# First operands made in halves on two engines, and a scaling of the third tile behind the last tile's first y addition: a two-layer hybrid decoder on one NeuronCore

## The chip, the cores and the metric

The kernel runs on one core of one Trainium2 chip. The metric is the device time of one execution in microseconds (us); lower is better.

## What is computed

Two layers work on x, 512 tokens of 1024 features in float32. Each layer normalises x, projects it with one wide matrix into eight groups of columns, runs a gated linear recurrence (HGRN2, 8 heads of 128) on some groups and a causal sliding-window attention (16 query heads of 64, 2 key/value heads, window 128, a learned sink per head) on others, gates both with SiLU, projects the joined heads back, and adds the normalised result to x:

```python
h = rms_norm(x, g_pre)
proj = jnp.einsum('bsd,de->bse', h, w_in)
q_h, f_h, i_h, z_h, q_a, k_a, v_a, z_a = jnp.split(proj, SPLIT_POINTS, axis=-1)
o_h = hgrn2(q_h, f_h, i_h, lb)
o_h = rms_norm(o_h, g_head).reshape(B, S, HG_WIDTH) * jax.nn.silu(z_h)
...
o_a = sliding_window_attention(q_a, k_a, v_a, sinks) * jax.nn.silu(z_a)
y = jnp.einsum('bse,ed->bsd', jnp.concatenate([o_h, o_a], axis=-1), w_out)
return x + rms_norm(y, g_post)
```

## The kernel before

Tokens lie in four tiles of 128 (NT), features in eight pieces of 128 (KT). A float32 operand of a matmul is written as a high part, rounded to the fp32r type, and a low part, the rest; each product is made of three matmuls, high x high, low x high and high x low. For weights, ACT casts the piece to the high part (line 183) and DVE subtracts it to get the low part (line 184).

The program is written with a scheduler. It estimates when each instruction could start and orders each engine's instructions by it, except those wrapped in `pin`, which keep the order in which the code gives them. So an edit in one place can change the order in another. Beside it, `later(n, ...)` puts a piece of code behind n steps of the projections (a step is three matmuls, line 295), and `merge` mixes attention or the recurrence with the projections' steps.

**The start.** The first work is the key/value projection of layer 0, in `first_kv` (line 1040). SP loads in turn the transposed x (tile xs, eight pieces of 128 features, called xk(k)) and its weights (tile raw, four pieces, each for two k). For each pair of k, `high` (ACT) scales xs by the gain gcol into hhi, `whigh` (ACT) casts the weights, `low` and `wlow` (DVE) make the low parts, and `kv(k)` issues twelve matmuls of 256 columns (line 1067): four token tiles for each of the three products. Ahead of them three warm-up matmuls run on a tile of ones (line 1044; the tile u in the profile). Later the rotated keys, tile b, are copied on ACT (line 476) and transposed on PE (line 492).

**Attention** (lines 548 to 635) makes, for sixteen steps, scores on PE (559, 572), masks them and takes the maximum on DVE (577, 579), then the negated maximum negm (583), exponentials on ACT (590), sums and their reciprocal on DVE (594, 595), the scaling of the probabilities s on POOL (597), transposes on PE (603), masks on POOL (615), values on PE (629), and an addition into oa on DVE (635).

**The end.** The last projection of the last layer makes y for each token tile in two halves of 512 columns; in the last tile the second half is cut in two pieces of 256. For each piece DVE adds the matmuls' result to y (line 912), ACT squares it and sums the squares (954), and, for the first half, POOL multiplies y by the gain (956); for the second half DVE makes that product, yg, which is the tile s in the profile (961). When a tile's pieces are done, DVE adds up the sums (951, 354), POOL takes the reciprocal root r (356), and DVE scales and adds both halves to x (973, tile a), each followed by its store to the output (974, on SP, for one piece of the last tile on ACT). The function is `final` (line 932). The additions of line 912 carry a high priority for the scheduler.

## Time and profile before

| | |
|---|---|
| time, median of 3 runs | 908.9 us (907.81 to 909.1) |
| the profiled execution's own time | 907.05 us |
| its span | 905.3 us |
| granted TensorE clock, mean | 0.999 |
| PE busy | 893.1 us, 99% of the span |
| DVE, ACT, POOL busy | 652.1, 471.7, 255.4 us |
| moved by DMA | 102.82 MB, mean 114 GB/s |

The span is the time between the first and the last event of the profiled execution. PE is the matmul engine, PEld its weight loads, DVE, ACT and POOL the vector, scalar and GpSimd engines, SP the engine that issues most transfers. A row of the timeline gives the start and the duration in us, the engine, the line of the kernel, the operation, the tile written and those read, and, in brackets, how long the engine was idle just before and what released it. An operation named x2 or x8 stands for that many in one row. The durations of PE's rows are modelled and overlap; the spacing of their starts is what a matmul takes.

### The profile page before, as it was taken

The page shows a single profiled execution, that of the slowest core. Times are in us where ns is not written, and L with a number is a line of the kernel's source. Part 1 is how long each engine was busy: PE and PEld are TensorE (multiplying, and loading weights), DVE is VectorE, ACT ScalarE, POOL GpSimd, SP SyncE. Part 2 cuts the span into 40 slices and gives each one's busy share as a digit, 9 for nine tenths or more (in the row PEclk, how much of TensorE's full clock was granted, in tenths as well). Part 3 has the DMA queues.
Part 4 walks back from the last instruction along what each step waited for, and adds up shares of the span by engine and source line. Part 5 has one row for each costly group of instructions (what it writes and reads, how often), then busy time and mean ns, then how long its engine had stood idle before and what let it go on. Part 6 is the DMA issues. An engine that isn't in the chain of part 4 may idle for free.

```text
span 905.3 us, 18588 instructions
## 1 busy us (share of the span) xinstructions
PE 893.1 (99%) x7206; PEld 746.8 (83%) x7206; DVE 652.1 (72%) x1179; ACT 471.7 (52%) x1067; POOL 255.4 (28%) x233
## 2 busy tenths in 40 slices
PE   9999999999999999999999999999999999999997
PEld 7788888888888878888888888888888888888885
DVE  5878987989666885555787787877767557666556
ACT  6636767654656323534453376686346463145242
POOL 0135544204313123020332344550134121230102
PEclk9999999999999999999999999999999999999999
DMA  8783712332222222434356556222422322223413
GB/s 307 225 219 123 204 48 70 105 94 84 72 82 74 91 82 60 129 122 128 99 176 187 150 154 173 65 73 86 116 73 60 105 69 84 72 71 99 135 35 140
DMA packets 57145, 102.82 MB, mean 114 GB/s; under 512 B 6625, under 2 KB 9185, under 8 KB 57057
## 3 DMA queue, kind: packets, MB, share of 16 engines
q1 hardware_dynamic: 56768, 101.50, 37.0%
q8 instruction: 57, 0.93, 0.4%
q14 instruction: 32, 0.25, 0.1%
q10 hardware_dynamic: 288, 0.14, 0.1%
HBM read 89.03 MB, written 12.58 MB: 112 GB/s over the span
## 4 chain that ended last, share of the span: by engine, by line
PE 87%; DVE 6%; issue 3%; ACT 2%; POOL 1%; DMA 0%; POOLq 0%; DVEq 0%; ACTq 0%
PE pj L295 71%; PE ac L629 3%; PE sc L572 2%; PE sc L770 2%; PE ac L839 2%; PE sc L603 1%; PE ac L842 1%; PE ac L826 1%; DVE wlo L184 1%; PE sc L892 1%; PE sc L559 1%; PE sc L814 1%; PE ac L711 1%; DVE a L973 1%; DVE y L912 0%
## 5 line engine op out<-in xcount | busy, mean ns | idle before, releaser
L183 ACT CAST whi<-raw 128x512 fp32r<-128x512 f32 x256 | 155.5, 620 | 123.1 <-PE pj L295 112.4
L184 DVE TENSOR_TENSOR wlo<-raw,whi 128x512 fp32r<-128x512 f32 x253 | 182.0, 737 | 41.7 <-ACT whi L183 40.3
L295 PE MATMUL pj<-hhi,wlo 128*128 128x512 f32 x512 | 202.3, 396 | 0.0
L295 PE MATMUL pj<-hhi,whi 128*128 128x512 f32 x512 | 199.9, 390 | 0.0
L295 PE MATMUL pj<-hlo,whi 128*128 128x512 f32 x512 | 199.5, 390 | 0.0
L295 PE MATMUL pj<-whi,ops 128*128 128x512 f32 (+1 forms) x520 | 172.8, 395 | 0.2 <-DVE ops L872 0.2
L295 PEld LDWEIGHTS pj<-whi,ops 128*128 128x128 f32 x520 | 97.2, 188 | 19.8 <-DVE ops L872 0.6
L295 PEld LDWEIGHTS pj<-hhi,whi 128*128 128x128 f32 x512 | 96.1, 188 | 20.6
L295 PEld LDWEIGHTS pj<-hhi,wlo 128*128 128x128 f32 x512 | 96.2, 188 | 19.4
L295 PEld LDWEIGHTS pj<-hlo,whi 128*128 128x128 f32 x512 | 96.2, 188 | 19.0
L295 PE MATMUL pj<-whi,hlo 128*128 128x512 f32 x256 | 102.9, 404 | 0.0
L295 PE MATMUL pj<-wlo,ops 128*128 128x512 f32 (+1 forms) x260 | 100.8, 388 | 0.5 <-ACT ops L871 0.5
L295 PE MATMUL pj<-wlo,hhi 128*128 128x512 f32 x256 | 100.3, 392 | 0.3 <-DVE wlo L184 0.3
L295 PE MATMUL pj<-whi,hhi 128*128 128x512 f32 x256 | 100.2, 391 | 0.0
L789 POOL TENSOR_TENSOR k<-k,tot 128x512 f32<-128x512 f32 x40 | 58.3, 1480 | 108.3 <-PE sc L770 51.9
L590 ACT ACTIVATE s<-sc,negm 128x128 f32<-128x128 f32 x128 | 45.5, 368 | 36.9 <-DVE negm L583 34.7
L295 PEld LDWEIGHTS pj<-wlo,ops 128*128 128x128 f32 x260 | 49.0, 188 | 9.6 <-ACT ops L871 0.9
L295 PEld LDWEIGHTS pj<-whi,hhi 128*128 128x128 f32 x256 | 48.0, 188 | 10.3
L295 PEld LDWEIGHTS pj<-wlo,hhi 128*128 128x128 f32 x256 | 48.3, 189 | 8.6 <-DVE wlo L184 0.8
L295 PEld LDWEIGHTS pj<-whi,hlo 128*128 128x128 f32 x256 | 48.2, 188 | 8.0
L788 DVE TENSOR_TENSOR q<-q,tot 128x512 f32<-128x512 f32 x40 | 37.4, 946 | 20.3 <-PE sc L774 10.9
L597 POOL TENSOR_TENSOR s<-s,sums 128x512 f32<-128x512 f32 x32 | 35.2, 1100 | 51.6 <-DVE sums L595 27.7
(211 smaller groups left out, 1392.0 us busy)
## 6 DMA issues: line engine op xcount, KB each, us to landing
raw<-in_win_dram SPq DMA_DIRECT2D x192, 256.0 KB, 2.7
raw<-in_wout_dram SPq DMA_DIRECT2D x64, 256.0 KB, 2.7
stack<-rot SPq DMA_DIRECT2D x16, 512.0 KB, 3.4
qs<-stack SPq DMA_DIRECT2D x32, 256.0 KB, 4.6
xs<-in_xt_dram SPq DMA_DIRECT2D x8, 256.0 KB, 5.3
raw<-in_wkv_dram SPq DMA_DIRECT2D x8, 256.0 KB, 3.6
a<-in_x_dram SPq DMA_DIRECT2D x8, 256.0 KB, 3.7
x_mid<-a SPq DMA_DIRECT2D x8, 256.0 KB, 3.3
```

The source lines that it names most:

```text
L183: keep(nc.scalar.copy(hi, v))
L184: keep((nc.gpsimd if i in on_pool and i % 2 else nc.vector).tensor_tensor(lo, v, hi.bitcast(F32), op=ALU.subtract))
L295: nc.tensor.matmul(u.o, lhsT=u.sta(k, u.w)[i], rhs=u.mov(k, u.w)[j], start=(n == 0), stop=(n == len(u.list) - 1))
L559: pin(nc.tensor.matmul(S[:, h * P:(h + 1) * P], lhsT=q[:, h, t_], rhs=kst[v][p][:, 0:P], start=(h == 0 and p == 0), stop=(h == 3 and p == 1)))
L572: pin(nc.tensor.matmul(S[:, h * 256:(h + 1) * 256], lhsT=q[:, 2 * hp_ + h, t_], rhs=kst[v][p][:, (n - 1) * P:(n + 1) * P], start=(h == 0 a ...
L590: nc.scalar.activation(pt[:, h * P:(h + 1) * P], cur[h], AF.Exp, bias=negm[:, h:h + 1], scale=SCALE, accum_out=sums[:, h:h + 1])
L597: nc.gpsimd.tensor_tensor(pv, pv, sums.unsqueeze(2).broadcast_to([P, 4, P]), op=ALU.mult)
L629: pin(nc.tensor.matmul(U, lhsT=vst[v][:, blk, :], rhs=d, start=(i == 0), stop=(i == len(terms) - 1)))
L770: pin(nc.tensor.matmul(L[32 * b:32 * b + 32, c:c + 16], lhsT=k[:, o_ + 32 * b:o_ + 32 * b + 32], rhs=qv[:, blk:blk + qu, 1, :], start=True ...
L788: nc.vector.tensor_tensor(qv[:, :, 1, :], qv[:, :, 1, :], tv[:, :, 0].unsqueeze(2).broadcast_to([P, 2 * nb, hh]), op=ALU.mult)
L789: nc.gpsimd.tensor_tensor(kv_[:, :, 0, :], kv_[:, :, 0, :], tv[:, :, 1].unsqueeze(2).broadcast_to([P, 2 * nb, hh]), op=ALU.mult)
L839: pin(nc.tensor.matmul(O[:, c], lhsT=A[:, c], rhs=vs(j, n), start=(n == 0), stop=False))
```

## The change

At the start, for k = 0 alone: hhi is made in two halves of 256 tokens by DVE (`tensor_scalar`), the weights' high part in two halves of 256 columns by ACT. For the first pair of k, the order of the matmuls is high x high of both k, and then the other two products of each. The warm-up is two matmuls of 512 columns, not two and a half, and reads a tile of ones of 128 columns repeated four times; that tile is filled first on DVE, ahead of mhalf. At the end, for the third tile (tt == NT - 2) of the last layer, the second scaling and its store are put behind five further steps with `later`, and pinned.

```diff
-            for i, (c, v, e, w) in enumerate(parts):
+            def put(i, c, v, e, w):
                 xs = xt[c][:, e:e + w]
-                (pin if not last else lambda ins: ins)(nc.vector.scalar_tensor_tensor(xs, v[:, e:e + w], r, xs, op0=ALU.mult, op1=ALU.add))
+                (pin if not last or (tt == NT - 2 and i) else lambda ins: ins)(nc.vector.scalar_tensor_tensor(xs, v[:, e:e + w], r, xs, op0=ALU.mult, op1=ALU.add))
...
+            for i, part in enumerate(parts):
+                if last and tt == NT - 2 and i:
+                    later(5, None, lambda e=(i, *part): put(*e))
+                else:
+                    put(i, *part)
...
+    ones = tmp("u")
+    nc.vector.memset(ones[:, 0:P], 1.0)
     mhalf = const.tile([P, 4], F32, name="mhalf")
...
-    ones = tmp("u")
-    nc.vector.memset(ones, 1.0)
...
-        for n in (512, 512, 256):
-            pin(nc.tensor.matmul(warm[:, 0:n], lhsT=ones[:, 0:P], rhs=ones[:, 0:n], start=True, stop=True))
+        for _ in range(2):
+            pin(nc.tensor.matmul(warm, lhsT=ones[:, 0:P], rhs=ones[:, 0:P].unsqueeze(1).broadcast_to([P, 4, P]), start=True, stop=True))
...
-        def kv(k):
-            for i, j in ((0, 0), (1, 0), (0, 1)):
+        def kv(k, pairs=((0, 0), (1, 0), (0, 1))):
+            for i, j in pairs:
...
+        conv[0] = tuple(big.tile([P, 512], F32R, tag="v", name="wkv", bufs=8) for _ in range(2))
+        for c in (slice(0, 256), slice(256, 512)):
+            pin(nc.vector.tensor_scalar(hhi[:, 0, c], xk(0)[:, c], gcol[:, 0:1], None, op0=ALU.mult))
+            pin(nc.scalar.copy(conv[0][0][:, c], raws[0][:, c]))
         for j in range(KT // 2):
-            high(2 * j)
-            whigh(j)
+            if j:
+                high(2 * j)
+                whigh(j)
             low(2 * j)
             high(2 * j + 1)
             wlow(j)
             low(2 * j + 1)
-            kv(2 * j)
-            kv(2 * j + 1)
+            if j:
+                kv(2 * j)
+                kv(2 * j + 1)
+            else:
+                for k in range(2):
+                    kv(k, [(0, 0)])
+                for k in range(2):
+                    kv(k, [(1, 0), (0, 1)])
```

The scheduler's order changes in three stretches: at the start, between the first projections and the middle of layer 0's attention, and at the end. Elsewhere, and on SP throughout, it is the same.

PE, where the rotated keys are transposed (line 492; pj is the PSUM tile of a projection, the numbers name single tiles). Before:

```order
L295 MATMUL pj_481<-hhi_121,whi_398 128x512
L295 MATMUL pj_543<-hhi_121,wlo_405 128x512
L295 MATMUL pj_543<-hlo_122,whi_404 128x512
L492 MATMUL sc2_80<-ident_110,b_498 128x128 x4
L492 MATMUL sc0_78<-ident_110,b_498 128x128 x4
L295 MATMUL pj_543<-hhi_121,whi_404 128x512
L295 MATMUL pj_543<-hhi_121,wlo_411 128x512
```

The same place of the changed kernel, in which all tile numbers from here on are one higher:

```order
L295 MATMUL pj_482<-hhi_121,whi_399 128x512
L295 MATMUL pj_544<-hhi_121,wlo_406 128x512
L295 MATMUL pj_544<-hlo_122,whi_405 128x512
L295 MATMUL pj_544<-hhi_121,whi_405 128x512
L492 MATMUL sc2_80<-ident_110,b_499 128x128 x4
L492 MATMUL sc0_78<-ident_110,b_499 128x128 x4
L295 MATMUL pj_544<-hhi_121,wlo_412 128x512
```

The projection's high x high matmul has moved ahead of the transposes; its weights are those of the matmul before it.

DVE, in the attention stage of layer 0, near 88 to 93 us of the profile (sc are score tiles, mx, negm, ds and sums the small values of a step, wlo a low weight part). Before:

```order
L583 SCALAR_TENSOR_TENSOR negm<-mx,nsnk 128x4
L184 TENSOR_TENSOR wlo<-raw,whi 128x512
L586 TENSOR_TENSOR ds<-snk,negm 128x4
L342 TENSOR_TENSOR a<-sc_80,a 128x512
L577 COPY_PREDICATED sc_78<-masks,sc_78 128x2x128
L184 TENSOR_TENSOR wlo<-raw,whi 128x512
L579 TENSOR_REDUCE mx<-sc_78 128x2
L577 COPY_PREDICATED sc_79<-masks,sc_79 128x2x128
L594 TENSOR_TENSOR sums<-sums,es 128x4
L635 TENSOR_TENSOR oa<-ac_82,u 64x2x128
L579 TENSOR_REDUCE mx<-sc_79 128x2
L595 RECIPROCAL sums<-sums 128x4
```

And in the changed kernel:

```order
L184 TENSOR_TENSOR wlo<-raw,whi 128x512
L583 SCALAR_TENSOR_TENSOR negm<-mx,nsnk 128x4
L635 TENSOR_TENSOR oa<-ac_81,u 64x2x128
L586 TENSOR_TENSOR ds<-snk,negm 128x4
L342 TENSOR_TENSOR a<-sc_80,a 128x512
L184 TENSOR_TENSOR wlo<-raw,whi 128x512
L577 COPY_PREDICATED sc_78<-masks,sc_78 128x2x128
L594 TENSOR_TENSOR sums<-sums,es 128x4
L579 TENSOR_REDUCE mx<-sc_78 128x2
L577 COPY_PREDICATED sc_79<-masks,sc_79 128x2x128
L595 RECIPROCAL sums<-sums 128x4
L635 TENSOR_TENSOR oa<-ac_82,u 64x2x128
```

A wlo has moved ahead of negm, and the reciprocal ahead of the addition into oa and of the second maximum.

DVE at the end of the program (y the result, s the product yg, ss the sums of squares, r the root of the third tile). Before:

```order
L973 SCALAR_TENSOR_TENSOR a<-y,r_9996,a 128x512
L973 SCALAR_TENSOR_TENSOR a<-s,r_9996,a 128x512
L912 TENSOR_TENSOR y<-pj,y 128x512
L912 TENSOR_TENSOR y<-pj,y 128x256
L961 TENSOR_TENSOR s<-y,b 128x256
L912 TENSOR_TENSOR y<-pj,y 128x256
L951 TENSOR_TENSOR ss<-ss 128x1
```

In the changed kernel:

```order
L973 SCALAR_TENSOR_TENSOR a<-y,r_9997,a 128x512
L912 TENSOR_TENSOR y<-pj,y 128x512
L973 SCALAR_TENSOR_TENSOR a<-s,r_9997,a 128x512
L912 TENSOR_TENSOR y<-pj,y 128x256
L961 TENSOR_TENSOR s<-y,b 128x256
L912 TENSOR_TENSOR y<-pj,y 128x256
L951 TENSOR_TENSOR ss<-ss 128x1
```

The third tile's second scaling has changed places with the last tile's first y addition; nothing else has moved here.

## The prediction

> **What bounds the kernel now.** The page first: its span and its first part.
>
> ```profile
> span 905.3 us, 18588 instructions
> PE 893.1 (99%) x7206; PEld 746.8 (83%) x7206; DVE 652.1 (72%) x1179; ACT 471.7 (52%) x1067; POOL 255.4 (28%) x233
> ```
>
> PE is busy in 893.1 of 905.3 us. A change that removes no large matmul can only move the 12 us in which PE isn't busy, and waits that the pipelined records hide. So I read the chain that ended last, in order of time, and then who PE waits for.
>
> ```profile
> 26.83 3.64 DMA raw<-in_win_dram
> ...
> 42.87 1.09 PE sc L492 x8
> 43.96 14.12 PE pj L295 x62
> ```
>
> ```profile
> PE sc L492 <- ACT b L476: 0.8, 1, 0.8
> ...
> PE sc L572 <- ACT s L590: 0.5, 2, 0.3
> ```
>
> Up to 42.87 the chain runs through transfers and the small engines; from there it is PE's stream nearly without a break (62 matmuls in 14.12, 0.23 each), and at the very end, shown further down, it leaves PE for DVE, ACT and POOL. In the waits each row gives total, times and longest: before the L492 transposes PE waits 0.8 us once, behind attention's exponentials 0.5 in two waits. These are the places to watch. The timeline shows the first.
>
> ```profile
> 41.70 0.39 PE L295 MATMUL pj<-hlo,whi 128*128 128x512 f32 x1
> ...
> 42.19 0.62 ACT L476 COPY b<-b 128x512 f32<-128x512 f32 x1 [2.02 <-DVE b L475]
> ...
> 42.87 1.09 PE L492 MATMUL sc<-ident,b 128*128 128x128 f32 x8 [0.78 <-ACT b L476]
> ```
>
> PE stands still for 0.78 us until ACT's copy of b is done. Whatever PE gains before 41.70 lengthens this wait, and up to 0.78 us of PE's lateness shortens it, as long as b's own chain stays where it is.
>
> **The first operands.** PE weight loads and ACT in the first 10 us.
>
> ```profile
> 1.53 0.50 PEld L1044 LDWEIGHTS sc<-u 128*128 128x128 f32 x2 [1.53 <-DVE u L1035]
> ...
> 3.40 0.34 PEld L1044 LDWEIGHTS sc<-u 128*128 128x128 f32 x1 [0.52 <-issue]
> ...
> 4.26 0.34 PEld L1044 LDWEIGHTS sc<-u 128*128 128x128 f32 x1 [0.52 <-issue]
> ...
> 4.59 0.62 ACT L1058 CAST wkv<-raw 128x512 fp32r<-128x512 f32 x1
> ...
> 5.03 0.19 PEld L1044 LDWEIGHTS sc<-u 128*128 128x128 f32 x1 [0.43 <-issue]
> ...
> 5.26 0.62 PEld L1067 LDWEIGHTS ac<-wkv,hhi 128*128 128x128 f32 x4
> ...
> 7.04 0.72 ACT L1050 ACTIVATE hhi<-xs,gcol 128x512 fp32r<-128x512 f32 x1 [1.03 <-DMA xs<-in_xt_dram]
> ...
> 7.73 1.23 PEld L1067 LDWEIGHTS ac<-wkv,hhi 128*128 128x128 f32 x8
> 7.75 0.62 ACT L1058 CAST wkv<-raw 128x512 fp32r<-128x512 f32 x1
> ...
> 9.37 1.03 PEld L1067 LDWEIGHTS ac<-wkv,hhi 128*128 128x128 f32 x8
> ```
>
> Today the first kv matmul waits for the whole cast of wkv, 4.59 to 5.21. In halves, beside hhi on DVE, the first half is there after some 0.42 us (the 128x256 square on ACT, in the last block of rows below), so PE starts near 5.0, a quarter of a microsecond sooner. That doesn't last. ACT makes hhi of k=1 after both casts, 4.6 + 2 x 0.42 + 0.72 = 6.2; then 20 of the first 24 matmuls remain, at 0.12 each (eight loads in 1.03, so (1.03 - 0.19) / 7). They end at 8.6. The next four need hhi of k=2, which waits for its transfer until 7.04, and wkv's second piece, cast right behind it by 8.37; the eight loads from 7.73 take 1.23 and not 1.03 because they meet that. So PE goes on at 8.4 to 8.6 either way: between nothing and 0.2 us later. The DVE halves of hhi cost 0.43 each at most (the 128x256 product on DVE, 897.78 below) and run while wkv's piece is still under way; what follows them on DVE is due only behind the first eight matmuls. The shorter warm-up, two instructions for two and a half, frees about 0.9 us that PE then spends waiting. All of it lies ahead of 41.70, with 0.78 us of wait as cover: I take 0, bounds 0 and, should b's chain be disturbed too, +0.2 and -0.2.
>
> **The order that moves with it.** One 512-column matmul that stood behind the L492 transposes now stands before them, its operands already used by the matmul before it. It fills 0.23 us of the 0.78 (the spacing above): -0.23. The bounds are -0.23 and 0, the latter if b comes later by as much. In the attention stage DVE's order changes in a few places. This is the one where PE waits.
>
> ```profile
> 88.02 0.68 DVE L184 TENSOR_TENSOR wlo<-raw,whi 128x512 fp32r<-128x512 f32 x1
> ...
> 91.86 0.41 DVE L635 TENSOR_TENSOR oa<-ac,u 64x256 f32<-64x256 f32 x1
> ...
> 92.52 0.16 DVE L595 RECIPROCAL sums<-sums 128x4 f32<-128x4 f32 x1
> ```
>
> ```profile
> 92.85 1.04 POOL L597 TENSOR_TENSOR s<-s,sums 128x512 f32<-128x512 f32 x1 [3.20 <-DVE sums L595]
> ```
>
> ```profile
> 93.48 0.39 PE L295 MATMUL pj<-whi,hhi 128*128 128x512 f32 x1
> 93.95 0.66 PE L603 MATMUL sc<-ident,s 128*128 128x128 f32 x4
> ```
>
> The matmul at 93.48 leaves the array after 0.23, at 93.71; the transposes start at 93.95, when POOL's s is done (92.85 + 1.04 = 93.89): a hidden wait of 0.24. In the new order the reciprocal stands ahead of the oa addition and the reduction, worth 0.66 (91.86 to 92.52), more than the wait: -0.24. Against it, the 0.68 us wlo is now ahead of negm, so the exponentials start later; bound +0.45 (0.68 less the 0.24). I take -0.24, since the reciprocal in the row waits for DVE's own queue and not for ACT.
>
> **The end.** DVE, ACT and POOL over the last two tiles.
>
> ```profile
> 882.79 0.69 DVE L961 TENSOR_TENSOR s<-y,b 128x512 f32<-128x512 f32 x1
> ...
> 892.83 1.29 POOL L956 TENSOR_TENSOR y<-y,b 128x512 f32<-128x512 f32 x1 [2.95 <-ACT u L954]
> ...
> 893.68 1.00 DVE L961 TENSOR_TENSOR s<-y,b 128x512 f32<-128x512 f32 x1
> ...
> 896.06 0.75 DVE L973 SCALAR_TENSOR_TENSOR a<-s,r,a 128x512 f32<-128x512 f32 x1
> ...
> 896.73 1.02 DVE L912 TENSOR_TENSOR y<-pj,y 128x512 f32<-128x512 f32 x2
> ...
> 897.50 0.63 ACT L954 ACTIVATE u<-y 128x512 f32<-128x512 f32 x1 [3.05 <-DVE y L912]
> ...
> 897.78 0.43 DVE L961 TENSOR_TENSOR s<-y,b 128x256 f32<-128x256 f32 x1
> ...
> 898.31 1.27 POOL L956 TENSOR_TENSOR y<-y,b 128x512 f32<-128x512 f32 x1 [2.95 <-ACT u L954]
> 898.54 0.42 DVE L912 TENSOR_TENSOR y<-pj,y 128x256 f32<-128x256 f32 x1 [0.34 <-PE pj L295]
> 898.88 0.71 DVE L951 TENSOR_TENSOR ss<-ss 128x1 f32<-128x1 f32 x1
> 899.06 0.42 ACT L954 ACTIVATE u<-y 128x256 f32<-128x256 f32 x1 [0.29 <-DVE y L912]
> 899.38 0.19 ACT L954 ACTIVATION_READ_ACCUMULATOR u<-y 128x1 f32 x1
> ...
> 899.85 0.15 DVE L354 SCALAR_TENSOR_TENSOR s<-ss 128x1 f32<-128x1 f32 x1
> ```
>
> The third tile's scaling a<-s (896.06) now follows the y addition (896.73). The products it adds are ready: only 24 matmuls of 256 columns, 24 x 0.12, lie between them and PE's end near 898.5, so they were done by 895.7. The addition starts at 896.06 and everything it releases 0.67 sooner: the square at 896.83, POOL's y at 897.64 to 898.91. DVE's total is the same, so L961 of 256 columns is still due at 897.78. Here the rows warn. Where POOL multiplies y, DVE's L961 takes 1.00 and not 0.69: it ends at 894.68, 0.56 after POOL's end at 894.12, as if its 512 columns had only then begun; and L951, one column, lasts 0.71, until POOL's end at 899.58. The addition L912, with one operand in PSUM, takes its plain 0.42 amid POOL's y (898.54). So in these rows a DVE operation with both operands in SBUF stands still while POOL works. The SBUF page of the Trainium skill (section "SBUF: two separate sides") says it as a lock: of such a DVE operation and a POOL one, the first to start has the port pair and the other fully blocks. The trace agrees, with 0.71 us for one column; by that rule the side that starts second pays, and the sum below is what it comes to.
>
> Before, POOL's y met L951, and L354 began at 899.85. After, it meets L961, due 0.14 us after POOL starts: L961 ends at 898.91 + 0.28 = 899.2, and the last y addition, which came at 898.54 when PE was done, comes near 899.1. From its start to the end of the square's readout took 1.03 (898.54 to 899.57), so L354 begins at about 900.15: +0.30. What follows (root on POOL, three scalings, the last store) is as before. Nothing waits behind the moved scaling but these DVE steps; its store moves 0.67 later on SP, well ahead of the last tile's. Bounds: -0.25 if POOL and DVE didn't meet (L354 right behind the readout at 899.57), +0.6 if all of the 0.58 us by which the addition comes later stayed.
>
> **Sum:** 0 - 0.23 - 0.24 + 0.30 = -0.17. The profiled execution took 907.05 us, its span and 1.75 around it, so it would take 906.9. It lies 1.85 under the median of the three runs, 908.9; on that scale 908.7. The parts' bounds added, -0.92 and +1.25, make 908.0 to 910.2 on it. About 0.2%, or 1.8 us, is what a measurement of this kernel can tell from no change.
>
> **The rivals.**
>
> *A, faster by the whole cover:* the end meets no POOL operation (-0.25), the L492 wait goes whole because b comes sooner (-0.78), and the waits behind the exponentials go (-0.5): -1.5, or 907.4. For it: the order moves at all these places. Against: b's chain is untouched, and DVE and POOL overlap unless POOL slips by 0.14 us. 0.13.
>
> *B, slower through attention:* the wlo of 0.68 us that DVE now does ahead of negm at several steps delays exponentials, sums, POOL's s and the transposes. Where a step has no slack PE pays up to 0.68. It decides from the third such step on: 3 x 0.68 + 0.30 - 0.23 = +2.1, or 911.0. For it: at 93.71 PE already waits. Against: that wait is one of few, and the same order brings the reciprocal forward. 0.08.
>
> *C, the clock:* the loads show PE slow at first, 0.34 up to 4.26, then 0.19 at 5.03, 3.5 us after its first matmul. While slow, a 512-column pass takes 0.43 (two in 3.40 to 4.26), so 0.21 for 256 columns and not 0.12. Warm-up ends sooner now, and PE pauses between 4.5 and 6.2. If the clock stayed low for all 24 first matmuls they'd cost 24 x 0.09 = 2.2 us more, of which the wait at 41.70 absorbs 0.55: +1.6 or, with the sum, 910.3; above 0.2% from about five matmuls more. Against: PE's pause of 0.78 before 42.87 slows nothing after it, the 62 matmuls from 43.96 keep 0.23. The Trainium skill's page "TensorE: Matmul & The Clock Gate" (section "What's actually happening") has the clock open after one busy window of about 3.4 us whose phase is free. By that rule a warm-up of two instructions may miss a full window, which is this rival; the trace agrees with the 3.5 us, and no run here shows the phase. 0.05.
>
> *D, no effect:* the end is as before and the waits merely shift: 908.9. For it: most edits lie under cover. 0.14. That the scaling is not moved is excluded by the order.
>
> **How the numbers follow.** The forecast has 0.60, A 0.13, B 0.08, C 0.05, D 0.14. The likeliest is the forecast's 908.7. The three runs of before spread over 1.3 us, so the range is the forecast's 908.0 to 910.2 taken down to A's 907.4: 907.4 to 910.2, with B, half of C and a few mishaps outside. Faster by over 0.2% needs A and more, such as waits that the records hide: 0.06. Slower: B and half of C, 0.10. Within: 0.84.
>
> **What would show it.** Right: PE's first kv load near 5.0, but PE at k=2 still at 8.4 to 8.6; the wait before L492 near 0.55 or less; transposes near 94 without a gap; L961 of 256 columns lasting over 1 us beside POOL's y, and the last y addition waiting for DVE, some 0.5 us, and no longer for PE. Wrong: a slow weight load after 5.5, more PE waits behind exponentials between 60 and 110, or a last L354 that starts less than 1.31 us after PE's last release (898.54 to 899.85 now).

## The result, and where the time went

| | before | after |
|---|---|---|
| median, same chip, 12 runs each | 907.9 us (906.95 to 909.1) | 909.52 us (908.57 to 911.18) |
| ratio after to before | | 1.0021, 95% interval 1.0014 to 1.0028 |
| the profiled execution's own time | 907.05 us | 908.58 us |
| its span | 905.3 us | 906.9 us |

The change makes the kernel slower by 1.6 us in the median, 1.3 to 2.5 us by the interval; the two profiled executions differ by 1.53. The forecast of 908.7 us came from a loss at the end and two gains ahead of it. The loss at the end came within 0.04 us of the forecast; of the two gains the one in attention was outweighed several times over by a loss in the same place. (In the experiment called e3 below, two of the twelve executions took 2303 and 4339 us; its ratio leaves them out.) First the first part of the changed kernel's profile page, against the first fence of the prediction.

```profile
PE 894.4 (99%) x7204; PEld 746.4 (82%) x7204; DVE 653.1 (72%) x1181; ACT 471.9 (52%) x1067; POOL 255.1 (28%) x233
```

PE has two rows fewer (one warm-up matmul, which is listed as two) and is listed as busy for 1.3 us more; its rows can run on through short waits, as one further down does. So the sums don't show the loss. The waits of PE in the changed kernel (total, times, longest) do:

```profile
PE sc L572 <- ACT s L590: 1.2, 3, 0.7
...
PE sc L492 <- ACT b L476: 0.5, 1, 0.5
```

The wait before the L492 transposes fell from 0.8 to 0.5, as forecast. The waits behind attention's exponentials grew from 0.5 in two to 1.2 in three. To place the loss, take the same work of PE in both kernels and read when it starts. PE in the changed kernel:

```profile
4.94 1.83 PE L1073 MATMUL ac<-wkv,hhi 128*128 128x256 f32 x8
...
17.16 0.40 PE L295 MATMUL pj<-hhi,wlo 128*128 128x512 f32 x1
...
42.84 1.09 PE L492 MATMUL sc<-ident,b 128*128 128x128 f32 x8 [0.53 <-ACT b L476]
...
66.40 0.60 PE L603 MATMUL sc<-ident,s 128*128 128x128 f32 x4
...
94.54 0.39 PE L295 MATMUL pj<-whi,hhi 128*128 128x512 f32 x1
94.77 0.60 PE L603 MATMUL sc<-ident,s 128*128 128x128 f32 x4
...
899.47 0.28 PE L295 MATMUL pj<-whi,ops 128*128 128x256 f32 x1
```

The same landmarks in the kernel before, as far as the prediction doesn't show them:

```profile
17.16 0.40 PE L295 MATMUL pj<-hhi,wlo 128*128 128x512 f32 x1
...
66.67 0.60 PE L603 MATMUL sc<-ident,s 128*128 128x128 f32 x4
...
898.22 0.28 PE L295 MATMUL pj<-whi,ops 128*128 128x256 f32 x1
```

The first projection matmul starts at 17.16 in both: the 0.33 us by which the first kv matmul comes sooner (4.94, was 5.27) is gone by then. L492 starts at 42.84 (42.87), now with one matmul more done ahead of it. At 66.40 (66.67) both kernels have the same work behind them, and the changed one is 0.27 ahead. The transposes that stood at 93.95 stand at 94.77, and PE's last matmul 1.25 later, 899.47 against 898.22. All of this lies in the attention of layer 0: at the recurrence's first products the distance is 1.32, and it no longer grows. From 0.27 ahead to 1.32 behind is a loss of 1.6 us in attention. What PE waits for near 90 us, in DVE, POOL, ACT and PE of the changed kernel:

```profile
87.18 1.09 POOL L615 TENSOR_SCALAR_AFFINE_SELECT pcur<-a 128x1024 fp32r<-128x1024 f32 x1
...
87.89 0.93 DVE L184 TENSOR_TENSOR wlo<-raw,whi 128x512 fp32r<-128x512 f32 x1 [0.32 <-ACT whi L183]
...
88.22 1.54 POOL L615 TENSOR_SCALAR_AFFINE_SELECT pprev<-a 128x1024 fp32r<-128x1024 f32 x1
...
88.74 1.04 DVE L583 SCALAR_TENSOR_TENSOR negm<-mx,nsnk 128x4 f32<-128x4 f32 x1
...
89.81 0.37 ACT L590 ACTIVATE s<-sc,negm 128x128 f32<-128x128 f32 x1 [1.21 <-DVE negm L583]
```

And the same step in the kernel before:

```profile
87.00 1.09 POOL L615 TENSOR_SCALAR_AFFINE_SELECT pcur<-a 128x1024 fp32r<-128x1024 f32 x1
...
87.87 0.23 DVE L583 SCALAR_TENSOR_TENSOR negm<-mx,nsnk 128x4 f32<-128x4 f32 x1
...
88.04 1.61 POOL L615 TENSOR_SCALAR_AFFINE_SELECT pprev<-a 128x1024 fp32r<-128x1024 f32 x1
88.32 0.37 ACT L590 ACTIVATE s<-sc,negm 128x128 f32<-128x128 f32 x1
```

The new order puts wlo ahead of negm. Read the ends, start plus duration. POOL's pcur ends at 88.27; wlo, plain duration 0.68, only then gets on and ends at 88.82; pprev, plain duration 1.09, is listed with 1.54; and negm, four columns wide, stands for 1.04 and ends at 89.78, 0.02 after pprev's 89.76. In the kernel before, negm slipped in between the two mask products and was done at 88.10. So the exponentials start at 89.81 instead of 88.32, 1.49 later, not 0.68 later, and PE stands for the better part of a microsecond. The timeline of PE there, after, shows it: the value product at 89.63 takes 0.23, the next row starts at 90.67.

```profile
89.63 0.39 PE L629 MATMUL ac<-pprev,vst 128*128 128x512 f32 x1
90.67 0.74 PE L572 MATMUL sc<-kst,qs 128*128 128x256 f32 x4 [0.66 <-ACT s L590]
```

Last, the end of the changed kernel, DVE, POOL and ACT, against the last fence of the prediction:

```profile
898.58 0.42 DVE L912 TENSOR_TENSOR y<-pj,y 128x256 f32<-128x256 f32 x1
898.90 1.29 POOL L956 TENSOR_TENSOR y<-y,b 128x512 f32<-128x512 f32 x1 [2.28 <-ACT u L954]
899.03 1.43 DVE L961 TENSOR_TENSOR s<-y,b 128x256 f32<-128x256 f32 x1
...
900.39 0.41 DVE L912 TENSOR_TENSOR y<-pj,y 128x256 f32<-128x256 f32 x1
...
901.44 0.16 DVE L354 SCALAR_TENSOR_TENSOR s<-ss 128x1 f32<-128x1 f32 x1 [0.18 <-ACT u L954]
```

L961 begins 0.13 after POOL, lasts 1.43 instead of 0.43 and ends 0.27 after POOL's end at 900.19. The last y addition then comes at 900.39, though PE was done at 899.75. From PE's end to L354 it was 1.35 us (898.50 to 899.85) and is 1.69: 0.34 lost, 0.30 forecast.

### The profile page after: what moved, and what is told of

The parts are those of the page before. It is cut to its first block, busy times and chain, and to the rows that moved or that the text cites. A ratio compares the mean times of both kernels' runs of the same rounds, so it can differ in the third digit from the quotient of the medians.

```text
span 906.9 us, 18585 instructions
## 1 busy us (share of the span) xinstructions
PE 894.4 (99%) x7204; PEld 746.4 (82%) x7204; DVE 653.1 (72%) x1181; ACT 471.9 (52%) x1067; POOL 255.1 (28%) x233
## 4 chain that ended last, share of the span: by engine, by line
PE 88%; DVE 5%; issue 3%; ACT 2%; POOL 1%; DMA 0%; POOLq 0%; DVEq 0%; ACTq 0%
PE pj L295 71%; PE ac L629 3%; PE sc L572 3%; PE sc L770 2%; PE ac L839 2%; PE sc L603 1%; PE ac L842 1%; PE ac L826 1%; PE sc L892 1%; DVE wlo L184 1%; PE sc L559 1%; PE sc L814 1%; PE ac L711 1%; ACT s L590 0%; PE sc L774 0%
## 5 line engine op out<-in xcount | busy, mean ns | idle before, releaser
L295 PE MATMUL pj<-hhi,wlo 128*128 128x512 f32 x512 | 203.0, 396 | 0.0
L295 PE MATMUL pj<-hlo,whi 128*128 128x512 f32 x512 | 199.4, 390 | 0.0
L295 PE MATMUL pj<-hhi,whi 128*128 128x512 f32 x512 | 199.3, 390 | 0.0
L295 PE MATMUL pj<-whi,ops 128*128 128x512 f32 (+1 forms) x520 | 172.8, 395 | 0.2 <-DVE ops L872 0.2
L295 PEld LDWEIGHTS pj<-whi,ops 128*128 128x128 f32 x520 | 97.2, 188 | 19.8 <-DVE ops L872 0.6
L295 PEld LDWEIGHTS pj<-hhi,whi 128*128 128x128 f32 x512 | 96.1, 188 | 20.6
L295 PEld LDWEIGHTS pj<-hhi,wlo 128*128 128x128 f32 x512 | 96.2, 188 | 19.3
L295 PEld LDWEIGHTS pj<-hlo,whi 128*128 128x128 f32 x512 | 96.2, 188 | 19.0
L295 PE MATMUL pj<-whi,hlo 128*128 128x512 f32 x256 | 103.1, 404 | 0.0
L295 PE MATMUL pj<-wlo,ops 128*128 128x512 f32 (+1 forms) x260 | 100.8, 388 | 0.5 <-ACT ops L871 0.5
L295 PE MATMUL pj<-wlo,hhi 128*128 128x512 f32 x256 | 100.3, 392 | 0.3 <-DVE wlo L184 0.3
L295 PE MATMUL pj<-whi,hhi 128*128 128x512 f32 x256 | 100.2, 391 | 0.0
L295 PEld LDWEIGHTS pj<-wlo,ops 128*128 128x128 f32 x260 | 49.0, 188 | 9.6 <-ACT ops L871 0.9
L295 PEld LDWEIGHTS pj<-whi,hhi 128*128 128x128 f32 x256 | 48.1, 188 | 10.2
L295 PEld LDWEIGHTS pj<-wlo,hhi 128*128 128x128 f32 x256 | 48.3, 189 | 8.7 <-DVE wlo L184 0.8
L295 PEld LDWEIGHTS pj<-whi,hlo 128*128 128x128 f32 x256 | 48.2, 188 | 7.9
```

The source lines that it names most:

```text
L295: nc.tensor.matmul(u.o, lhsT=u.sta(k, u.w)[i], rhs=u.mov(k, u.w)[j], start=(n == 0), stop=(n == len(u.list) - 1))
```

## The experiments

The runs came in three groups of four, each with its own runs of the kernel before (medians 907.43, 907.66 and 907.31 us). Ratios are to these, that of the changed kernel to the 907.9 above. For orientation, some starts on PE in the profiled executions, as differences from the kernel before (L492 at 42.87, the recurrence's first products at 198.30, PE's end at 898.50) and how far L354 stands behind PE's end:

| kernel | ratio to before, 95% interval | L492 | recurrence | between the two | L354 behind PE's end |
|---|---|---|---|---|---|
| before | | | | | 1.35 |
| after | 1.0021 [1.0014, 1.0028] | -0.03 | +1.32 | +1.35 | 1.69 |
| e1 old warm-up | 1.0011 [1.0002, 1.0019] | +1.13 | +1.38 | +0.25 | 1.68 |
| e2 tail alone | 1.0007 [0.9998, 1.0015] | +0.33 | +0.26 | -0.07 | 1.68 |
| e3 warm-up alone | 1.0019 [1.0010, 1.0028] | +0.14 | +1.77 | +1.63 | 1.35 |
| e4 negm first | 1.0026 [1.0015, 1.0037] | +1.94 | +2.92 | +0.98 | 1.67 |
| e5 masks of one step quartered | 1.0015 [1.0006, 1.0023] | +2.87 | +3.57 | +0.70 | 1.68 |
| e6 all POOL products quartered | 1.0018 [1.0009, 1.0027] | +0.61 | +1.12 | +0.51 | 1.66 |
| e7 the same in before | 1.0015 [1.0006, 1.0024] | -0.21 | +1.23 | +1.44 | 1.35 |
| e8 halves and pair order alone | 1.0002 [0.9993, 1.0011] | +0.81 | +1.10 | +0.29 | 1.33 |
| e9 tail, no POOL product | 0.9997 [0.9988, 1.0006] | +0.46 | +0.47 | +0.01 | 1.09 |
| e10 halves alone | 1.0003 [0.9994, 1.0012] | +0.65 | +0.77 | +0.12 | 1.33 |
| e11 masks of two steps quartered | 1.0009 [1.0001, 1.0018] | +0.45 | +0.74 | +0.29 | 1.66 |
| e12 wlo ahead of negm in before | 1.0014 [1.0005, 1.0023] | +0.43 | +1.52 | +1.09 | 1.33 |

The column to read is "between the two", the loss from L492 on, in attention; L492 itself moves with the start, which varies from one execution to the next (below). In the kernels with the changed order (after, e4 to e6, e11) one projection matmul that stood behind L492 stands ahead of it, so for the same work their loss is about 0.25 larger than the column says: 1.6 and not 1.35 in the changed kernel. In e3 four matmuls have moved so. The kernels whose attention has the old order (e1, e2, e8 to e10) lie between -0.07 and +0.29: a difference of 0.3 can't be told from none.

### e1: the changed kernel with the old warm-up

```diff
-        for _ in range(2):
-            pin(nc.tensor.matmul(warm, lhsT=ones[:, 0:P], rhs=ones[:, 0:P].unsqueeze(1).broadcast_to([P, 4, P]), start=True, stop=True))
+        for n in (512, 512, 256):
+            pin(nc.tensor.matmul(warm[:, 0:n], lhsT=ones[:, 0:P], rhs=ones[:, 0:n], start=True, stop=True))
```

> The changed kernel with the old warm-up (three matmuls, the whole tile of ones, filled after mhalf); halves, matmul order of the first pair and the moved scaling stay. With that the attention stage has the order of before again. Theory T (the 1.6 us are 1.3 from one attention step, where a wlo now stands ahead of negm, and 0.3 from the end): the span is that of before + 0.3, about 905.6, ratio to before 1.0003; no wait over 0.5 us between 84 and 92. Rival S (the halves and the new matmul order at the start cost): it stays at before + 1.3 or more, ratio over 1.0014. Rival E (the end costs all): + 1.6.

Measured: 908.48 us. The warm-up enters the scheduler's estimates; with the old one it gives attention the order that it has in the kernel before, and attention's loss is 0.25 instead of 1.35. The rest of the way to L492, +1.13, is new. PE's waits in this kernel:

```profile
PE ac L1073 <- ACT hhi L1056: 1.6, 1, 1.6
```

PE waits 1.6 us for hhi of k=1, which the new order of the first matmuls asks for after four of them and not after twelve. Its xs landed late in this execution. e8 and e10 come back to it.

### e2: the edit at the end alone

```diff
+            def put(i, c, v, e, w):
...
+                if last and tt == NT - 2 and i:
+                    later(5, None, lambda e=(i, *part): put(*e))
```

> Before with the moved scaling alone; on all engines but for two rows on DVE the order is that of before. Theory T: + 0.3 us, ratio 1.0003, POOL's y beside L961 of 256 columns, which lasts over 1 us, L354 about 0.3 later relative to PE's end. Rival E: + 1.6, ratio 1.0018. Rival S: 0.

Measured: 908.16 us, a ratio that includes 1. Only two rows of DVE trade places, and L354 stands 1.68 behind PE's end, 0.33 more than before. This term of the sum stands.

### e3: the shorter warm-up alone

```diff
-        for n in (512, 512, 256):
-            pin(nc.tensor.matmul(warm[:, 0:n], lhsT=ones[:, 0:P], rhs=ones[:, 0:n], start=True, stop=True))
+        for _ in range(2):
+            pin(nc.tensor.matmul(warm, lhsT=ones[:, 0:P], rhs=ones[:, 0:P].unsqueeze(1).broadcast_to([P, 4, P]), start=True, stop=True))
```

> Before with the shorter warm-up alone (two matmuls that read 128 columns of ones four times). The scheduler's order in the attention stage changes: again a wlo ahead of negm at the second step of the second group, other places not quite as in the change. Theory T: + 1.0 to 1.4 us at that step, negm lasting about 1 us beside POOL, the first kv matmuls and the end as before; ratio 1.0011 to 1.0015. Rival C (the clock opens later): slow weight loads of 0.34 after 5.5 us, first kv matmuls later, + 1 to 2. Rival S or E: 0.

Measured: 909.24 us, nearly all of the loss from two instructions at 1.5 us that PE would have spent waiting, and more than the 1.0 to 1.4 expected. Its waits (the longest near 112, 0.5 us at this step) and the step near 88 us:

```profile
PE sc L572 <- ACT s L590: 1.8, 4, 0.8
```

```profile
88.11 1.54 POOL L615 TENSOR_SCALAR_AFFINE_SELECT pprev<-a 128x1024 fp32r<-128x1024 f32 x1
...
88.62 1.04 DVE L583 SCALAR_TENSOR_TENSOR negm<-mx,nsnk 128x4 f32<-128x4 f32 x1
```

Attention's order differs in places from that of the whole change, but wlo stands ahead of this negm here too, and negm ends with pprev again (89.66 and 89.65).

### e4: the changed kernel with that wlo behind negm

```diff
+            if i == 29:
+                def low():
+                    with tc.high_priority(170):
+                        pin(nc.vector.tensor_tensor(lo, v, hi.bitcast(F32), op=ALU.subtract))
+                behind.append(low)
...
+            if (l, g, n) == (0, 1, 1):
+                behind.pop()()
```

> The changed kernel, in which only that one wlo (weight piece 29) is held behind that step's negm; the rest of the order follows with small shifts. Theory T: the exponentials of the step start 1.2 to 1.5 us sooner, the wait of 0.8 near 90 is gone, the time is that of the change less 1.0 to 1.3, ratio to before 1.0003 to 1.0007. Rival M (many small shifts of the order cost, not this pair): less than 0.5 us comes back, ratio over 1.0013. Rivals S and E: nothing comes back.

Measured: 909.68 us, no better than the changed kernel. The wait near 90 is gone, but the scheduler moved other rows, and from 100 to 104 us PE falls behind by some 0.6 us once more. The next long negm of this kernel, with POOL:

```profile
100.92 1.04 POOL L607 TENSOR_TENSOR s<-s,sums 128x512 f32<-128x512 f32 x1 [5.75 <-DVE sums L605]
...
101.25 0.73 DVE L591 SCALAR_TENSOR_TENSOR negm<-mx,nsnk 128x4 f32<-128x4 f32 x1
```

Here it is the scaling of s under which negm falls, and again it ends when POOL does, 101.98 and 101.96. So the cause need not be the one pair, as the first theory had it; it may be the meeting with POOL, wherever the order brings it about. In before, after and e1 to e4, 10 of the 96 negm in layer 0 last over 0.35 us, and each of these ends within 0.02 us of the end of a POOL instruction. That is theory P of the following runs. Such a meeting can be changed with the order left alone, by cutting POOL's instruction.

### e5: the changed kernel, the masks of one step in four pieces

```diff
+                for e in range(0, 8, 2) if (l, g, n) in [(0, 0, 3)] else [slice(0, 8)]:
+                    e = e if isinstance(e, slice) else slice(e, e + 2)
+                    m = e.stop - e.start
...
-                                        pattern=[[0, 8], [-sg, P]], compare_op=ALU.is_ge, fill=0.0,
+                                            pattern=[[0, m], [-sg, P]], compare_op=ALU.is_ge, fill=0.0,
```

> The changed kernel; GpSimd's two mask products of one step, the last tile of the first head group in layer 0, are made in four pieces of 256 columns each instead of one of 1024; VectorE, ScalarE and TensorE have the very order of the changed kernel. Theory P (a VectorE operation with both operands in SBUF stands until GpSimd's instruction ends, so the new order costs what is left of a GpSimd instruction): the negm at 88.74 that lasted 1.04 lasts 0.15 to 0.4 and ends by 89.1, not 89.78; the exponentials that started at 89.81 start 0.6 to 0.8 sooner; TensorE's wait of 0.8 near 89.9 shrinks to 0.2 or less; the later wait near 111.8 (0.3) stays. The last L354 0.5 to 0.8 sooner than in the changed kernel, median near 908.8, ratio to before 1.001. Rival O (the order alone costs: the product of 0.68 stands ahead of negm, whatever GpSimd does): negm may be short, but the wait stays at 0.6 or more and the ratio at 1.002.

Measured: 908.58 us. All rows of PE, DVE and ACT stand in the order of the changed kernel. DVE and ACT at that step (this execution started 2.9 us late, so 91.64 here is 88.74 there):

```profile
90.76 0.96 DVE L184 TENSOR_TENSOR wlo<-raw,whi 128x512 fp32r<-128x512 f32 x1 [0.32 <-ACT whi L183]
91.64 0.36 DVE L583 SCALAR_TENSOR_TENSOR negm<-mx,nsnk 128x4 f32<-128x4 f32 x1
...
92.03 0.37 ACT L590 ACTIVATE s<-sc,negm 128x128 f32<-128x128 f32 x1 [0.56 <-DVE negm L583]
...
92.49 0.40 PE L632 MATMUL ac<-pprev,vst 128*128 128x512 f32 x1
92.89 0.74 PE L572 MATMUL sc<-kst,qs 128*128 128x256 f32 x4
```

negm lasts 0.36 instead of 1.04 behind the same wlo, and PE goes from the value product to the scores in 0.40 where the changed kernel took 1.04 (89.63 to 90.67). The product itself takes 0.23, so the wait is 0.17 and was 0.81. Attention's loss falls from 1.35 to 0.70. Rival O is out: the order is unchanged, and most of the wait is gone.

### e6 and e7: all of POOL's attention products in four pieces, after and before

```diff
-            nc.gpsimd.tensor_tensor(pv, pv, sums.unsqueeze(2).broadcast_to([P, 4, P]), op=ALU.mult)
+            for h in range(4):
+                nc.gpsimd.tensor_tensor(pv[:, h], pv[:, h], sums[:, h:h + 1].broadcast_to([P, P]), op=ALU.mult)
```

The masks are cut at every step as in e5.

> The changed kernel; all of GpSimd's products of attention in both layers (the scaling by the reciprocal of the sums and the two mask products of each step) in four pieces each; the other engines' orders are those of the changed kernel. Theory P: no negm in layer 0 lasts over 0.45, the waits near 87, 90 and 112 (0.25, 0.8, 0.3) shrink to 0.3 in sum; from the transposes before L492 to the hgrn products 0.8 to 1.3 us less than in the changed kernel, about what the kernel before has; median 908.2 to 908.7, ratio to before 1.0003 to 1.001. GpSimd's busy time grows. Rival O: the waits stay, ratio 1.002. If GpSimd's pieces have a cost of their own that delays the value products, slower than the changed kernel: 1.003.

> The kernel before with the same quartering of GpSimd's attention products; the other engines' orders are those of the kernel before. Theory P: the negm at 72.01 and 93.16 (0.71 and 0.75) fall to 0.45 or less, the wait of 0.24 at 93.5 goes; 0.2 to 0.5 us faster, ratio 0.9995 to 0.9998, which is at the edge of what can be told. Rival O: 1.000. If the quartered kernel before is as fast as the quartered changed one but for 0.3 at the end, the order no longer matters, which is P.

Measured: 908.9 and 908.96 us. No negm lasts over 0.41, so P's row came true, but its times did not. In e6 attention's loss is 0.51, near what P said; in e7 attention got 1.44 slower. PE's waits in e7, and POOL at the step that costs most:

```profile
PE sc L604 <- POOL s L598: 1.0, 2, 0.6
```

```profile
92.93 2.44 POOL L598 TENSOR_TENSOR s<-s,sums 128x128 f32<-128x128 f32 x4 [2.20 <-DVE sums L595]
```

Cut in four, POOL's scaling of s lasts 1.48 instead of 1.04 in sum where nothing meets it. Here it lasts 2.44: a wlo of DVE from 93.31 and a rot from 94.44, each with two operands in SBUF, get in beside the third and the fourth piece, which last 0.85 and 0.92 instead of 0.40, and PE's transposes wait for them. So the case that the expectation named for e6, a cost of the pieces, struck e7, in good part because the gaps between the pieces let DVE in ahead of POOL. The pair doesn't show what it was made for; that the order no longer matters, P's stronger claim, isn't shown.

### e8 and e10: the halves with and without the new order of the first matmuls

e8 has both in the kernel before; e10 leaves out the second hunk:

```diff
+        for c in (slice(0, 256), slice(256, 512)):
+            pin(nc.vector.tensor_scalar(hhi[:, 0, c], xk(0)[:, c], gcol[:, 0:1], None, op0=ALU.mult))
+            pin(nc.scalar.copy(conv[0][0][:, c], raws[0][:, c]))
...
+                for k in range(2):
+                    kv(k, [(0, 0)])
+                for k in range(2):
+                    kv(k, [(1, 0), (0, 1)])
```

> The kernel before with the first operands in halves and the new order of the first 24 matmuls alone; the warm-up and the end as before; the attention stage has the order of before. S0 (the start is worth nothing): first L295 matmul at 17.1 to 17.3 when the transfers land as in the kernel before, ratio 1.000. S1 (the new order needs hhi of k=1 four matmuls sooner, so a transfer of xs that lands late now stops TensorE, as in the run with the old warm-up where it waited 1.6 us for it): a wait of TensorE for hhi near 5.7 to 7.5 in some executions; median 0.3 to 0.8 us slower, ratio 1.0003 to 1.0009. S2 (a gain of the halves hidden by the rest): 0.2 to 0.3 faster, 0.9997.

> The kernel before with the first operands in halves alone; the first 24 matmuls keep their order (twelve of k=0, then twelve of k=1), the warm-up and the end are those of before. S1 (the new pair order, not the halves, makes the start late in executions in which the transfer of xs for k=1 lands late): TensorE does not wait for hhi of k=1 by more than 0.3 us as long as that hhi is done by 7.3; the first L295 matmul at 17.0 to 17.4, the L492 transposes within 0.3 of 42.87; ratio 0.9995 to 1.0003. S0 (order and halves are both without effect, the late starts are chance): the same late starts, 0.5 to 1 us, in this run as in those with the new order.

Measured: 908.05 us (1.0002) and 907.8 us (1.0003), both the same as before. e8 shows the wait for hhi of k=1 that S1 named, 0.5 us; e10 doesn't. But e10's start was late as well: the first L295 matmul at 18.21 and not near 17.2. The weight loads of PE in e10 show another cause:

```profile
5.54 1.19 PEld L1067 LDWEIGHTS ac<-wkv,hhi 128*128 128x128 f32 x4
6.61 0.97 PEld L1067 LDWEIGHTS ac<-wkv,hlo 128*128 128x128 f32 x4
7.46 1.10 PEld L1067 LDWEIGHTS ac<-wkv,hhi 128*128 128x128 f32 x8
```

The four loads from 6.61 take 0.97 here, and eight at full speed would take 1.03: PE is slow until about 7.6, and was until about 5.0 in the profiled execution of before. Of the kernels whose start is that of before to the letter, e2, e9 and e12 have their first L295 matmul 0.72 to 0.82 later than it, e7 0.11. So the one profiled execution of before, whose 907.05 us is near the fastest of all its runs, stands for the good end. Neither S0 nor S1 is decided: L492 lies between 42.66 and 43.52 in seven executions with the old order of the first matmuls, and between 42.84 and 45.74 in seven with the new one, while e8 and e10 are not told apart by their ratios.

### e9: the edit at the end without POOL's last product

```diff
-                nc.gpsimd.tensor_tensor(y[:, 0], y[:, 0], hT2["gpost"][0], op=ALU.mult)
+                if not last or tt < NT - 1:
+                    nc.gpsimd.tensor_tensor(y[:, 0], y[:, 0], hT2["gpost"][0], op=ALU.mult)
```

The kernel leaves out the gain of the first half of the last tile.

> The kernel before with the tail edit alone, and for the last tile GpSimd's product of y with the gain (L956) is left out, so that part of the computation is missing. Theory P (a VectorE operation with both operands in SBUF stands until GpSimd is done): the L961 of 256 columns lasts 0.4 to 0.5, not 1.43, and the last L354 stands 1.3 to 1.4 us behind TensorE's last release, as in the kernel before (1.35), not 1.68 as with the tail edit and the product. Ratio to before 0.9997 to 1.0002. Rival (the earlier addition merely shifts VectorE's own row, GpSimd has no part in it): L961 stays above 0.9 and L354 1.6 us or more behind.

Measured: 907.41 us, ratio 0.9997. DVE at its end:

```profile
898.36 0.43 DVE L962 TENSOR_TENSOR s<-y,b 128x256 f32<-128x256 f32 x1
899.12 0.42 DVE L912 TENSOR_TENSOR y<-pj,y 128x256 f32<-128x256 f32 x1 [0.34 <-PE pj L295]
899.47 0.15 DVE L951 TENSOR_TENSOR ss<-ss 128x1 f32<-128x1 f32 x1
```

With POOL idle the 256-column product takes 0.43 and not 1.43, L951 0.15 and not the 0.71 of before, and the last addition waits for PE again. L354 stands 1.09 behind PE's end, sooner than the 1.3 to 1.4 expected, since L951 is free as well.

### e11: the masks of two steps in four pieces

The edit of e5 with the steps (0, 0, 3) and (0, 1, 2).

> The changed kernel with GpSimd's mask products in four pieces at two steps of layer 0: the last tile of the first head group, as before, and the third tile of the second, whose products at 105.3 to 107.5 stretch the VectorE product (1.10 at 106.93) ahead of the exponentials that TensorE waits for near 111.8. Theory P: the wait near 90 is 0.2 or less, as with the one step quartered, and the 0.3 near 111.8 is gone too; from the transposes before L492 to the hgrn products 0.8 to 1.1 us less than in the changed kernel; median 908.2 to 908.7 beside 907.7 before, ratio 1.0006 to 1.0013. If the second wait stays (0.3), its cause is the order of VectorE's row and not GpSimd.

Measured: 908.06 us. Attention's loss is 0.29 instead of 1.35 (for the same work about 0.55 instead of 1.6), with the order of the changed kernel on the three other engines. PE at the second place in the changed kernel, and in e11:

```profile
111.78 1.44 PE L572 MATMUL sc<-kst,qs 128*128 128x256 f32 x8
```

```profile
111.54 1.12 PE L572 MATMUL sc<-kst,qs 128*128 128x256 f32 x8
```

The first row hides a wait of 0.3, between the first four of its eight matmuls and the rest; in the second it is gone. So that wait too came from POOL, through a wlo of 1.10 beside pprev.

### e12: one wlo ahead of one negm, in the kernel before

```diff
+            if (l, g, n) == (0, 1, 1):
+                tc.add_manual_dep(ins.ins, ahead[0], mybir.DependencyInfo(mybir.DependencyClass.NoSync, mybir.DependencyReason.DATA), reason="order")
```

Here `ahead` holds the name of that wlo, and `ins` is negm.

> The kernel before with one VectorE product of a weight piece (L184) held ahead of the negm of the first tight step (second head group, second tile, layer 0), as it stands in the changed kernel; start, warm-up and end are those of before. Theory P: the product begins near 87.9, negm comes 0.6 later, lands under GpSimd's pprev product and lasts 0.9 to 1.1 instead of 0.23; the exponentials that started at 88.32 start near 89.7; TensorE waits 0.5 to 0.8 us there; at the hgrn products 0.6 to 1.2 us later than the kernel before; ratio 1.0007 to 1.0013. Rival O2 (the place of one product means nothing, the loss came from the changed order at large): negm below 0.5, no new wait near 90, ratio 1.000 within 0.0004.

Measured: 908.85 us. DVE, POOL, ACT and PE at the step:

```profile
88.35 0.69 DVE L186 TENSOR_TENSOR wlo<-raw,whi 128x512 fp32r<-128x512 f32 x1
88.45 1.54 POOL L621 TENSOR_SCALAR_AFFINE_SELECT pprev<-a 128x1024 fp32r<-128x1024 f32 x1
...
88.97 1.04 DVE L587 SCALAR_TENSOR_TENSOR negm<-mx,nsnk 128x4 f32<-128x4 f32 x1
...
90.04 0.37 ACT L596 ACTIVATE s<-sc,negm 128x128 f32<-128x128 f32 x1 [1.20 <-DVE negm L587]
...
91.42 0.74 PE L576 MATMUL sc<-kst,qs 128*128 128x256 f32 x4 [0.74 <-ACT s L596]
```

The same picture as in the changed kernel, made by one instruction's place: negm 1.04, ended with pprev (90.01 and 89.99), PE waiting 0.74, and 1.09 us lost in attention. Rival O2 is out. Later rows moved too, and a second negm (115.03, 0.82) met the scaling of s; not all of the 1.09 is this one step's. At the next transposes (95.21, before 93.95) 0.8 us of it is lost.

No version that computes the whole beat the kernel before. The parts of the change that gain, the matmul ahead of L492 and the earlier reciprocal, hang on the order that brings the meeting.

## Why the prediction was wrong, step by step

**The start, forecast 0.** Right for the execution that was profiled: 4.94 for the first kv load (5.0 forecast), 8.52 for k=2 (8.4 to 8.6), 17.16 against 17.16. The reason given was only half of it. It priced hhi of k=1 at 6.2 with its transfer landed; in six of the seven profiled executions with the new order the transfer or ACT was later than PE, which waited 0.5 to 1.8 us. In two of them rival C happened. In e4 PE had not got fast before the wait, and the four loads from 9.09 still take 0.97. In e5 it was at full speed after the wait and then slow once more. e5's weight loads:

```profile
7.59 0.53 PEld L1076 LDWEIGHTS ac<-wkv,hhi 128*128 128x128 f32 x4 [2.00 <-ACT hhi L1059]
...
9.07 0.97 PEld L1076 LDWEIGHTS ac<-wkv,hlo 128*128 128x128 f32 x4
9.93 1.82 PEld L1076 LDWEIGHTS ac<-wkv,hhi 128*128 128x128 f32 x8
```

And the row of that stretch in a table by windows, busy times of the engines first; the last three numbers are the granted clock, the DMA engines' share and GB/s:

```profile
8.88:12.29 3.41, 3.41 (x19) 3.41 (x18) 3.33 (x6) 3.32 (x5) 0.00 (x0) 0.50 1.06 386
```

For 3.41 us the granted clock is 0.50, and four loads take 0.97 instead of 0.53; on PE that is 1.5 us of the 2.2 that C priced for all 24 matmuls. The mean over the span, 0.997, hides it, and of the slow phase at the very start the column shows nothing: it reads 1.00 from 4.00 to 5.40, where the loads still take 0.33. How much of the median such starts make is open: e8 and e10 give 0.2 and 0.3 us for the start by their ratios, with an interval of 0.8 either way, and the 1.53 us between the two profiled executions are accounted for without it.

**The matmul ahead of L492, forecast -0.23.** Right: the wait fell from 0.78 to 0.53, and at 66.40 PE is 0.27 ahead.

**Attention, forecast -0.24 with a bound of +0.45.** This is the step that failed. The gain is there: the hidden wait at 93.7 is gone, and the transposes at 94.77 follow the matmul at 94.54 without a gap (0.23). But the sentence "Against it, the 0.68 us wlo is now ahead of negm, so the exponentials start later; bound +0.45" priced wlo at its plain duration and negm at nothing. negm ended 1.68 later (88.10 to 89.78) and the exponentials began 1.49 later, since ACT's own rows covered 0.2. Together with the places below attention cost 1.6 for the same work (1.35 by the table's column) instead of saving 0.24. The rule that would have priced it stands in the next part of the prediction, drawn from the rows of the end: a DVE operation with both operands in SBUF stands still while POOL works. It was applied to L961 and not to negm, and POOL's mask products at 87.0 to 89.7 are not among the prediction's rows. e12 shows that this one place alone loses 0.8 us; e5 and e11 show that the same order costs 0.70 and 0.29 by the column, about 0.25 more for the same work, when POOL's long instructions are cut at this step, and at this step and one more.

The prediction also weighed one place only. Two more projection matmuls now stand ahead of the transposes at 78.75 (before 78.57), so attention's rows come 0.18 later, and PE has less left to do when it needs s: at 87.28 (87.10) it has stood 0.25 us for POOL's scaling (86.18 + 1.04 = 87.22). There the 0.27 that PE was ahead is gone and it is 0.18 behind; e5 and e11 keep this loss. Some 0.3 more goes near 112. No run tests the loss at 87.28 apart.

**The end, forecast +0.30.** Right in size and in mechanism: 0.34 in the changed kernel, 0.33 alone (e2), gone when POOL's product is left out (e9). L961 ended 0.27 after POOL, 0.28 forecast.

**The rivals.** B had the place and the kind of the loss, slower through attention's negm, but asked for three steps at 0.68; one step with 1.49 did about half of it (0.8 in e12), and other places the rest. Its sentence against, that the same order brings the reciprocal forward, was true and worth 0.24. A and D are out.

**The sum.** From -0.27 at 66.40 attention adds 1.6 (the recurrence's products at +1.32); PE's end stands at +1.25, and the end adds 0.34: L354 is 1.59 later, the execution's own time 1.53, the median 1.6. Three of the four terms came out, 0, -0.27 and 0.34; in place of attention's -0.24 stands +1.6. That the measured 909.52 still lies between 907.4 and 910.2 is luck: the scale, the median of three runs (908.9), lay 1.0 above that of the twelve (907.9), and from 907.9 the same range ends at 909.2.

## What to carry to other kernels

When an edit reorders an engine, price each instruction that moves at the time it would then start, with what the neighbour on the shared path is doing at that moment, and not at its plain duration; a four-column operation cost more here than the 512-column one that was put ahead of it. Look at the places where the kernel before doesn't wait but nearly does, since there the new order has no cover. And where a scheduler sets the order, a change of two cheap instructions can move a stage 80 us later: read the new order there first, and try the edit's parts apart.

## What the runs showed of the hardware

A DVE operation that reads two operands from SBUF and a POOL product or mask that reads SBUF didn't run side by side; the second waited for the first, and they took turns: pcur, wlo, pprev, negm in the changed kernel, with ten long negm in six kernels (before, after, e1 to e4) ending within 0.02 us of POOL. In the kernel before, a row that nobody waited for, ds at 88.63, took the same 1.04. A POOL memset, which only writes, doesn't hold DVE: in the kernel before one takes 0.96 from 608.78, and the two wlo from 608.56 take 1.30 together, as two do with POOL idle (1.31 from 14.07). The page "SBUF — State Buffer" of the Trainium skill (section "Who interferes with whom") says that a DVE instruction with two SBUF inputs contends with a POOL one that reads SBUF and not with one that only writes it, that the contention is an exclusive lock, and that the order of issue decides which side is blocked. These runs agree, with 0.36 us for negm when POOL's pieces are short and 1.04 when they are long.

Cutting POOL's work has its own price. A mask product of 1024 columns takes 1.09; two pieces of 256 took 0.77 beside no such DVE work, so four make about 1.5, an estimate. The scaling of 512 columns takes 1.04 whole and 1.48 in four, and 2.44 where DVE's rows got in between the pieces (e7).

PE's slow first microseconds ended at 5.0 in one execution (before) and at 7.6 in another with the same warm-up (e10). In e5, after a pause of 1.8 us, PE went on at full speed for 1.3 us and was then slow once more, at a granted clock of 0.50 for 3.41 us; in e1 a pause of 1.6 us at the same place was followed by no slow stretch, and four loads take 0.55 or less from then on. The page "TensorE: Matmul & The Clock Gate" (section "What's actually happening") of the Trainium skill has the gate decide by windows of about 3.4 us whose phase is free, and has it close after an idle one. The 3.41 us and the differing ends agree with it, but in e5 the slow stretch followed a pause of about half such a window; what share of a window must be idle, these runs don't show.
